# A causal convolution of four taps as one chain of three DVE instructions, on one Trainium2 core

## The chip, the core and the metric

One core of a Trainium2 chip runs the whole program. PE (TensorE) multiplies matrices into PSUM, DVE (VectorE), ACT (ScalarE) and POOL (GpSimd) work elementwise beside it, and SP (SyncE) issues most of the DMAs. Each engine takes its own instructions strictly in the order in which they were written, and semaphores hold an instruction until what it reads is there. The metric is the device time of one execution in microseconds (us).

## The reference

A trunk of two layers over 1024 frames of 1024 channels in float32. Layer 0 is chunked attention, layer 1 a gated DeltaNet, and a squared-ReLU MLP follows each. The part that matters here is the input of the DeltaNet layer: q, k and v (8 heads of 128 channels each) pass a depthwise causal convolution of four taps and a SiLU.

```python
CONV_K = 4
def causal_conv(x, w):
    """Depthwise causal conv. x: (B,S,Ch), w: (K,Ch); last tap hits the current frame."""
    S = x.shape[1]
    xp = jnp.pad(x, ((0, 0), (CONV_K - 1, 0), (0, 0)))
    y = xp[:, 0:S] * w[0]
    for j in range(1, CONV_K):
        y = y + xp[:, j:j + S] * w[j]
    return y
...
def gated_deltanet(h, w_in, conv_w, a_log, dt_bias, head_norm, w_o):
    proj = h @ w_in
    ...
    qkv = jax.nn.silu(causal_conv(qkv, conv_w))
    q, k, v = jnp.split(qkv, 3, axis=-1)
    ...
    o = chunk_gated_delta_rule(q, k, v, g, beta)
```

`chunk_gated_delta_rule` solves a unit lower triangular system in each chunk of 64 frames and then carries a 128x128 state through 16 chunks per head, one after the other.

## The kernel before

Activations lie transposed, channels on the 128 partitions and frames along the free dimension, in two halves of 512 frames (`HB`). A float32 product is made of three fp32r matmuls with operands split into a high and a low part (`whi`, `wlo`, `xs`), so a dense output tile of 128 channels and 512 frames takes 24 matmuls into a PSUM bank `acc`.

The DeltaNet stage (`deltanet`, `dn_run`) goes through a list of dense jobs: k of heads 0 to 7, then q and v of heads 0 to 2, then z, q and v by turns, the last z, and two panels of the output projection (`o`). Each of the 32 jobs ahead of the output projection has 48 matmuls. After every dense matmul `dn_run` calls `turn`, which steps other tasks where their inputs are ready: `dn_evac` (this change), `dn_blocks` (the k by k products `U` of a head), `dn_solves` (the triangular solves, four heads at a time, 31 steps of a product `ft` and a reduction `fz` on DVE), `dn_inverses`, `dn_prep_keys`, `dn_prep_values`, `dn_prep_queries`, `dn_scans` (16 dependent steps per head: PE makes `s`, DVE makes `vn`, PE, DVE makes the next state `st`), `dn_outs` and `dn_reload`.

Which task steps when is decided while the program is built, by a planned clock (`Clock`): each instruction is charged a planned cost (on DVE, 0.08 + 512/850 us for one scalar_tensor_tensor of 512 columns), a task becomes ready at the planned end of its last step, and tasks whose priority is 1 or more wait while DVE or ACT is planned more than 2 us ahead of PE. So a change of one task's instructions moves the others' places in all queues. Ring buffers (`xp`, `cy`, `cz`, two of each) are taken and given back on the same clock.

`dn_evac` handles one half head. For q, k and v it scales the bank into `xp` (with three columns carried over from the first half), multiplies tap 3 into `y` (a `cy` tile) and tap 1 into `z` (a `cz` tile) on ACT, adds tap 2 to `y` and tap 0 to `z` on DVE, sums `y` and `z` on POOL, and applies SiLU on ACT into `k`, `qT` or `vT`. For k of heads 4 to 7 (`POOLED`) the division of work is another: POOL sums taps 3 and 1, ACT makes a third product (tap 0), DVE adds tap 2 alone, and POOL sums again. There are 48 half heads, 8 of them pooled.

All instructions of this stage are recorded through one wrapper at line 163, so the profile shows L163 for them, and they are told apart by the names of their tiles (`cy<-xp,convw` is an ACT product, `cy<-xp,convw,cy` a DVE tap, `cy<-cy,cz` the POOL sum). After the change that wrapper stands at line 162.

Of the kernel before, what the change touches and what calls it, by code (L numbers as in the profile page):

```python
# [10 lines left out]
AF = mybir.ActivationFunctionType  # L11
ALU = mybir.AluOpType
# [8 lines left out]
HB = 512  # L21
# [13 lines left out]
ATT = (3, 2, 0.5, 1, 1, 0.7, 0.6)  # L35
RINGS = {"pt": 2, "po": 2, "sp": 1, "pr": 6, "bias": 3, "thi": 4, "tlo": 3, "oh": 1, "ot": 2}
ENGINES = {"dn_solves": ("vector",), "dn_decays": ("scalar",)}
POOLED = (4, 5, 6, 7)


def wide(col, p, n):
# [166 lines left out]
class Trunk:  # L208
# [1862 lines left out]
    def dn_evac(self, c, h, half, ps):  # L2071

        nc = self.nc
        s = slice(half * HB, (half + 1) * HB)
        if c == "z":
            if half == 0:
                if h == 1:
                    yield from self.until("solve", 1)
                if h >= 2:
                    yield from self.until("out", h - 2)  # L2080
                self.heads[c, h] = self.dn_out_of(c, h)
            while (c, h) not in self.heads:
                yield
            t = self.heads[c, h][:, s]
            nc.vector.tensor_tensor(t, ps, self.R[:, s], ALU.mult)
            self.give("acc", ps)
            yield
            nc.scalar.activation(t, t, AF.Silu)
        else:
            w = self.convw[:, 8 * "qkv".index(c) + h]  # L2090
            xp = yield from self.take("xp")
            if half == 0:
                nc.vector.memset(xp[:, 0:3], 0.0)
            else:
                nc.vector.tensor_copy(xp[:, 0:3], self.edge[:, HB : HB + 3])
            self.edge = xp
            nc.vector.tensor_tensor(xp[:, 3 : 3 + HB], ps, self.R[:, s], ALU.mult)
            self.give("acc", ps)
            yield
            yt = yield from self.take("cy")  # L2100
            zt = yield from self.take("cz")
            y, z = yt[:, :HB], zt[:, :HB]
            nc.scalar.activation(y, xp[:, 3 : 3 + HB], AF.Copy, scale=w[:, 3:4])
            nc.scalar.activation(z, xp[:, 1 : 1 + HB], AF.Copy, scale=w[:, 1:2])
            yield
            if c == "k" and h in POOLED:
                nc.gpsimd.tensor_tensor(z, y, z, ALU.add)
                yield
                nc.scalar.activation(y, xp[:, 0:HB], AF.Copy, scale=w[:, 0:1])
                nc.vector.scalar_tensor_tensor(z, xp[:, 2 : 2 + HB], w[:, 2:3], z, ALU.mult, ALU.add)  # L2110
            else:
                nc.vector.scalar_tensor_tensor(y, xp[:, 2 : 2 + HB], w[:, 2:3], y, ALU.mult, ALU.add)
                nc.vector.scalar_tensor_tensor(z, xp[:, 0:HB], w[:, 0:1], z, ALU.mult, ALU.add)
            self.give("xp", xp)
            yield
            nc.gpsimd.tensor_tensor(y, y, z, ALU.add)
            self.give("cz", zt)
            yield
            if half == 0:
                for need in self.dn_room(c, h):  # L2120
                    yield from self.until(*need)
                self.heads[c, h] = self.dn_out_of(c, h)
            while (c, h) not in self.heads:
                yield
            nc.scalar.activation(self.heads[c, h][:, s], y, AF.Silu)
            self.give("cy", yt)
            self.silu_at = self.clock.at["scalar"]
        if half == 1:
            self.mark(c, h)
# [532 lines left out]
```

## Time and profile before

| what | value |
|---|---|
| three runs | 2573.45, 2576.89, 2579.90 us; median 2576.89 us |
| the profiled execution | 2579.18 us, of which the span from the first to the last instruction is 2577.4 us |
| PE | busy 2472.7 us, 96% |
| DVE | busy 1914.8 us, 74% |
| POOL | busy 1298.2 us, 50% |
| ACT | busy 1210.1 us, 47% |
| DeltaNet stage | about 1206 to 1860 us of the span |

Busy times are shares of the span over all stages, whose limits differ. PE's ends are modelled, so a busy PE isn't PE at its peak. A row of an engine's timeline has its start, its duration, the operation, the tiles (`out<-in`), the shape and a count; what stands in brackets is the idle time just ahead of it and what ended that. The chain of waits goes back from the last instruction, at each step to what released it.

### The profile page before, as it was taken

What the parts mean: (1) busy time and instruction counts of PE and PEld (TensorE: products, weight loads), DVE (VectorE), ACT (ScalarE), POOL (GpSimd) and SP (SyncE); (2) the same over time, 40 slices, a digit from 0 to 9 for tenths busy, and PEclk for the clock granted to TensorE, in tenths of its full rate; (3) what the DMA queues carried; (4) which work ended last, traced back from release to release, by engine and by line L of the source; (5) the groups of instructions that cost most, each with busy time, mean ns of one, the idle gap of its engine ahead of it and who ended that gap; (6) DMA issues with size and microseconds to landing.
All of it is one profiled execution on the core that took longest, in us unless ns stands there. A gap on an engine that the chain in (4) does not pass through costs nothing.

```text
span 2577.4 us, 36731 instructions
## 1 busy us (share of the span) xinstructions
PE 2472.7 (96%) x12638; PEld 2063.6 (80%) x12638; DVE 1914.8 (74%) x3297; ACT 1210.1 (47%) x2269; POOL 1298.2 (50%) x1090
## 2 busy tenths in 40 slices
PE   8999999999999999998888999999899999999997
PEld 6888888787888788886677788888787888787885
DVE  6665556677878788877578976666678787778877
ACT  6666567535555433334673333333335555433333
POOL 2444355515677476556464333332314766466656
PEclk9999999999999999999998999999999999999998
DMA  4222224424555976743343121122323555967742
GB/s 160 68 65 73 71 84 129 140 82 167 210 203 215 358 233 227 249 147 111 116 142 106 55 82 60 59 85 94 119 98 143 208 209 200 345 235 253 249 160 82
DMA packets 193082, 392.43 MB, mean 152 GB/s; under 512 B 54960, under 2 KB 61552, under 8 KB 192896
## 3 DMA queue, kind: packets, MB, share of 16 engines
q1 hardware_dynamic: 176048, 355.46, 41.0%
q10 hardware_dynamic: 16848, 34.63, 3.4%
q8 instruction: 100, 1.64, 0.3%
q14 instruction: 86, 0.70, 0.1%
HBM read 254.06 MB, written 127.57 MB: 148 GB/s over the span
## 4 chain that ended last, share of the span: by engine, by line
PE 61%; DVE 11%; DMA 3%; issue 3%; ACT 1%; POOL 1%; SPq 0%; ACTq 0%; DVEq 0%; POOLq 0%
PE y L1008 24%; PE z L1008 11%; PE acc L163 9%; PE acc L1008 6%; PE tp L163 4%; PE s L163 3%; DVE ft L163 2%; PE acc L279 1%; PE acc L277 1%; PE acc L278 1%; DVE x L1512 1%; DMA wraw<-in_w_up_dram 1%; DVE wlo L1014 1%; DVE fz L163 1%; DVE xs L393 1%
## 5 line engine op out<-in xcount | busy, mean ns | idle before, releaser
L163 PE MATMUL acc<-xs,whi 128*128 128x512 f32 x1808 | 633.9, 414 | 10.4 <-DVE xp L163 9.8
L163 PEld LDWEIGHTS acc<-xs,whi 128*128 128x128 f32 x1808 | 334.8, 192 | 60.0 <-DVE xp L163 6.1
L163 PE MATMUL acc<-xs,wlo 128*128 128x512 f32 x896 | 369.6, 413 | 2.1 <-POOL wlo L163 2.1
L1008 PE MATMUL y<-xs,whi 128*128 128x512 f32 x1008 | 312.0, 390 | 5.2 <-DVE x L1512 1.8
L163 POOL TENSOR_TENSOR wlo<-wraw,whi 128x512 fp32r<-128x512 f32 x126 | 167.7, 1331 | 246.3 <-ACT whi L163 197.3
L1023 POOL TENSOR_TENSOR s<-wraw 128x256 f32<-128x256 f32 (+1 forms) x93 | 89.4, 962 | 352.9 <-DVE a L1014 171.9
L1014 DVE TENSOR_TENSOR wlo<-wraw,whi 128x512 fp32r<-128x512 f32 (+1 forms) x182 | 209.4, 1151 | 27.3 <-ACT whi L1017 27.3
L1008 PEld LDWEIGHTS y<-xs,whi 128*128 128x128 f32 x1008 | 189.2, 188 | 47.1 <-DVE x L1512 2.6
L1017 ACT ACTIVATE whi<-wraw 128x512 fp32r<-128x512 f32 (+2 forms) x191 | 146.5, 767 | 123.8 <-PE y L1008 86.6
L1008 PE MATMUL y<-xs,wlo 128*128 128x512 f32 x504 | 197.0, 391 | 6.2 <-DVE wlo L1014 6.2
L1008 PE MATMUL y<-xs,a 128*128 128x512 f32 x732 | 189.0, 394 | 10.0 <-DVE x L1512 9.8
L1017 ACT ACTIVATE a<-s 128x256 fp32r<-128x256 f32 x122 | 63.8, 524 | 281.5 <-PE y L1008 141.7
L163 PEld LDWEIGHTS acc<-xs,wlo 128*128 128x128 f32 x896 | 172.6, 193 | 27.0 <-POOL wlo L163 2.5
L1512 DVE TENSOR_TENSOR x<-y,x 128x512 f32<-128x512 f32 x240 | 165.0, 688 | 36.8 <-PE y L1008 28.6
L1008 PEld LDWEIGHTS y<-xs,a 128*128 128x128 f32 x732 | 136.6, 189 | 44.5 <-DVE x L1512 14.2
L1008 PE MATMUL acc<-xs,whi 128*128 128x512 f32 x528 | 162.9, 390 | 0.0
L1008 PE MATMUL y<-xs,ahi 128*128 128x512 f32 x512 | 159.2, 392 | 0.7 <-ACT nt L1201 0.4
L1090 DVE TENSOR_TENSOR c<-c 128x512 fp32r<-128x512 f32 x112 | 132.8, 1203 | 28.5 <-POOL c L1020 28.5
L163 POOL TENSOR_SCALAR pr<-pr,rs 128x640 f32<-128x640 f32 (+4 forms) x128 | 88.1, 692 | 129.4 <-DVE rs L163 96.7
L1008 PE MATMUL z<-xs,whi 128*128 128x512 f32 x480 | 148.8, 391 | 0.0
L163 POOL TENSOR_TENSOR cy<-cy,cz 128x512 f32<-128x512 f32 x48 | 68.9, 1435 | 146.7 <-DVE cz L163 124.3
L163 DVE CUSTOM_DVE_ANT_0 pr<-sp,bias 128x640 f32<-128x640 f32 (+4 forms) x128 | 83.8, 655 | 63.8 <-PE sp L163 62.8
(340 smaller groups left out, 6295.2 us busy)
## 6 DMA issues: line engine op xcount, KB each, us to landing
xs<-gt SPq DMA_DIRECT2D x256, 256.0 KB, 4.9
gt<-c SPq DMA_DIRECT2D x112, 512.0 KB, 3.0
wraw<-in_w_up_dram SPq DMA_DIRECT2D x64, 512.0 KB, 3.5
wraw<-in_w_down_dram SPq DMA_DIRECT2D x64, 512.0 KB, 4.4
r<-gr SPq DMA_DIRECT2D x88, 256.0 KB, 3.4
wraw<-in_w_in_dram SPq DMA_DIRECT2D x32, 512.0 KB, 3.4
gr<-ssum ACTq DMA_DIRECT2D x62, 256.0 KB, 3.2
wraw<-in_w_qkv_dram SPq DMA_DIRECT2D x30, 512.0 KB, 3.4
```

The costliest lines, as they stand in the source:

```text
L163: return call(*args, **more)
L277: nc.tensor.matmul(ps, hi[:, k], xh, start=(k == 0), stop=False)
L278: nc.tensor.matmul(ps, hi[:, k], xl, start=False, stop=False)
L279: nc.tensor.matmul(ps, lo[:, k], xh, start=False, stop=(k == KT - 1))
L393: self.nc.vector.scalar_tensor_tensor(lo, x, w, hi.bitcast(F32), ALU.mult, ALU.subtract)
L1008: nc.tensor.matmul(ps, w[:, k], x, start=bool(first and f), stop=bool(last and e), skip_group_check=True)
L1014: self.nc.vector.tensor_tensor(lo, src, hi.bitcast(F32), ALU.subtract)
L1017: self.nc.scalar.activation(hi, src, AF.Copy)
L1023: self.nc.gpsimd.tensor_tensor(out, x, y, ALU.add)
L1090: nc.vector.tensor_tensor(t[z][:, HB:].bitcast(F32R), t[z][:, HB:], t[z][:, :HB], ALU.subtract)
L1512: nc.vector.tensor_tensor(x, ps, x, ALU.add)
```

## The change

A half head's convolution becomes one product on ACT (tap 3, into `cy`) and three scalar_tensor_tensor instructions on DVE that add taps 2, 1 and 0 to the same tile, each reading what the one ahead of it wrote. The second ACT product, the two sums on POOL and the special way of k's heads 4 to 7 go. `cz` isn't taken by the convolution any more (`dn_reload` still uses it).

```diff
-POOLED = (4, 5, 6, 7)
...
             yt = yield from self.take("cy")
-            zt = yield from self.take("cz")
-            y, z = yt[:, :HB], zt[:, :HB]
+            y = yt[:, :HB]
             nc.scalar.activation(y, xp[:, 3 : 3 + HB], AF.Copy, scale=w[:, 3:4])
-            nc.scalar.activation(z, xp[:, 1 : 1 + HB], AF.Copy, scale=w[:, 1:2])
-            yield
-            if c == "k" and h in POOLED:
-                nc.gpsimd.tensor_tensor(z, y, z, ALU.add)
-                yield
-                nc.scalar.activation(y, xp[:, 0:HB], AF.Copy, scale=w[:, 0:1])
-                nc.vector.scalar_tensor_tensor(z, xp[:, 2 : 2 + HB], w[:, 2:3], z, ALU.mult, ALU.add)
-            else:
-                nc.vector.scalar_tensor_tensor(y, xp[:, 2 : 2 + HB], w[:, 2:3], y, ALU.mult, ALU.add)
-                nc.vector.scalar_tensor_tensor(z, xp[:, 0:HB], w[:, 0:1], z, ALU.mult, ALU.add)
+            yield
+            for n in (2, 1, 0):
+                nc.vector.scalar_tensor_tensor(y, xp[:, n : n + HB], w[:, n : n + 1], y, ALU.mult, ALU.add)
             self.give("xp", xp)
-            yield
-            nc.gpsimd.tensor_tensor(y, y, z, ALU.add)
-            self.give("cz", zt)
             yield
```

Counted over the program, ACT loses 56 products (104 become 48) and 2 table loads (20 become 18), POOL loses 56 sums, and DVE gains 56 scalar_tensor_tensor (88 become 144).

Three places show how the order moves. The first is DVE at the start of the first solve, where the convolutions of k's last heads stand among the solve's steps (`ft`, `fz`) and the `U` products. Before:

```order
L163 TENSOR_TENSOR U_13195<-tp_13196,vT_12994 128x512
L163 TENSOR_TENSOR ft_13174<-fz_12321,fu_12320 128x9
L163 TENSOR_REDUCE fz_12321<-ft_13174 128x3
L163 TENSOR_TENSOR ft_13174<-fz_12321,fu_12320 128x16
L163 TENSOR_REDUCE fz_12321<-ft_13174 128x4
L163 TENSOR_TENSOR U_13195<-tp_13225,vT_12994 128x512
L163 SCALAR_TENSOR_TENSOR cz_13183<-xp_13160,convw,cz_13183 128x512
L163 TENSOR_TENSOR ft_13174<-fz_12321,fu_12320 128x25
```

And of the change:

```order
L162 TENSOR_TENSOR fu_12320<-fu_12320,ry_13096 128x1024
L162 SCALAR_TENSOR_TENSOR cy_13174<-xp_13156,convw,cy_13174 128x512 x3
L162 TENSOR_TENSOR ft_13210<-fz_12321,fu_12320 128x1
L162 TENSOR_REDUCE fz_12321<-ft_13210 128x1
L162 TENSOR_TENSOR U_13140<-tp_13217,vT_12997 128x512
L162 TENSOR_TENSOR ft_13210<-fz_12321,fu_12320 128x4
L162 TENSOR_REDUCE fz_12321<-ft_13210 128x2
```

Where one tap stood ahead of a solve step, three stand in a row. Counting the dense matmuls ahead of it in PE's order, the first solve's first step moves from 342 to 367 and its last from 541 to 594; the second solve's first step moves from 599 to 682, and the first head's first scan step from 613 to 691.

The second place is POOL over the same stretch (`wlo` is a weight's low part, `row` and `vT` hold decays to be masked). Before:

```order
L163 TENSOR_TENSOR wlo_12824<-wraw_12673,whi_12823 128x512
L163 TENSOR_TENSOR cz_12887<-cy_12886,cz_12887 128x512
L163 TENSOR_TENSOR wlo_12925<-wraw_12761,whi_12924 128x512
L163 TENSOR_TENSOR cz_12929<-cy_12928,cz_12929 128x512
L163 TENSOR_TENSOR row_12915<-row_12915,mask 128x512
L163 TENSOR_TENSOR cy_12886<-cy_12886,cz_12887 128x512
```

And of the change:

```order
L162 TENSOR_TENSOR wlo_12893<-wraw_12779,whi_12892 128x512 x2
L162 TENSOR_TENSOR row_12927<-row_12927,mask 128x512 x2
L162 TENSOR_TENSOR vT_12997<-vT_12997,mask 128x512 x2
L162 TENSOR_TENSOR wlo_13035<-wraw_12844,whi_13034 128x512 x2
```

Only weights and masks are left on POOL there.

The third place is PE at the end of the stage, where head 7 is scanned (`s`, with `vn`, `st`, `kd`, `WQ` and `qk`) beside the last dense matmuls (`acc`). Before:

```order
L163 MATMUL s_3767_17862<-st_17846,WQ_17613 128x128
L163 MATMUL acc_17844<-xs_11813,whi_17570 128x512 x2
L163 MATMUL acc_17844<-xs_11813,wlo_17571 128x512
L163 MATMUL acc_17844<-xs_11815,whi_17570 128x512 x2
L163 MATMUL acc_17844<-xs_11815,wlo_17571 128x512
L163 MATMUL s_3779_17887<-vn_12245,kd_17498 128x128
L163 MATMUL s_3767_17862<-vn_12245,qk_12251 128x128
L163 MATMUL acc_17844<-xs_11817,whi_17570 128x512 x2
L163 MATMUL acc_17844<-xs_11817,wlo_17571 128x512
```

And of the change:

```order
L162 MATMUL s_3736_17832<-st_17826,WQ_17582 128x128
L162 MATMUL s_3740_17840<-vn_12244,kd_17465 128x128
L162 MATMUL s_3736_17832<-vn_12244,qk_12251 128x128
L162 MATMUL s_3742_17852<-st_17846,WQ_17582 128x128
L162 MATMUL s_3743_17857<-vn_12245,kd_17465 128x128
L162 MATMUL s_3742_17852<-vn_12245,qk_12251 128x128
L162 MATMUL s_3745_17864<-st_17861,WQ_17582 128x128
```

Several scan steps now follow each other with no dense matmul between them. Head 7's scan begins behind 1530 dense matmuls instead of 1476, and 20 scan steps instead of 9 stand behind the 1536th.

## The prediction

> **What bounds the kernel now.** The chain of waits comes first, since it tells which engine's work ended last. Over the whole program:
>
> ```profile
> PE 61%; DVE 11%; DMA 3%; issue 3%; ACT 1%; POOL 1%; SPq 0%; ACTq 0%; DVEq 0%; POOLq 0%
> ```
>
> PE carries the program and DVE is second, with shares of 61% and 11%; ACT and POOL, which lose work here, have 1% each. Such shares are averages, so the next view is the busy time by stretches of the DeltaNet stage, to which the change is confined (columns: the stretch, its length, PE, PEld, DVE, ACT and POOL busy with their counts, PE's granted clock, the DMA share, GB/s):
>
> ```profile
> 1220.00:1420.00 200.00, 172.81 (x848) 143.13 (x847) 147.52 (x268) 114.29 (x201) 107.11 (x80) 0.91 0.41 121
> 1420.00:1540.00 120.00, 113.97 (x815) 96.13 (x814) 103.96 (x221) 45.03 (x91) 44.14 (x33) 1.00 0.22 66
> 1540.00:1820.00 280.00, 273.11 (x1883) 239.74 (x1882) 183.00 (x474) 105.18 (x233) 88.10 (x65) 0.99 0.23 75
> 1820.00:1860.00 40.00, 32.66 (x154) 25.36 (x153) 25.06 (x62) 15.20 (x31) 10.46 (x10) 0.96 0.45 151
> ```
>
> The reader is to see four limits. From 1220 to 1420 (k's jobs, the first solve) PE is idle for 27 of 200 us and runs at a clock of 0.91, which costs 9% of its 173 busy us, another 16: some 43 us are lost there, with no engine full. From 1420 to 1540 (the second solve) DVE is busy 87%. From 1540 to 1820 PE is the bound, 98% busy, and DVE has a third free. In the last 40 us PE waits again, for head 7's scan.
>
> What PE waits for in the first stretch is read from the waits of the stage (us in total, times, longest) and from single rows of PE:
>
> ```profile
> PE acc L163 <- DVE xp L163: 9.8, 2, 5.9
> 1363.52 0.63 ACT L163 ACTIVATE qT<-cy 128x512 f32<-128x512 f32 x1 [4.83 <-POOL cy L163]
> 1364.72 3.57 PE L163 MATMUL tp<-ones,nt 128*128 128x1 f32 x16 [3.43 <-ACT nt L163]
> 1368.73 0.63 PE L163 MATMUL acc<-xs,wlo 128*128 128x512 f32 x1
> 1369.15 1.05 PE L163 MATMUL acc<-xs,whi 128*128 128x512 f32 x2
> 1385.87 0.39 PE L163 MATMUL acc<-xs,wlo 128*128 128x512 f32 x1
> 1386.10 0.62 PE L163 MATMUL acc<-xs,whi 128*128 128x512 f32 x2
> 1395.13 2.07 PE L163 MATMUL tp<-qT,kn 128*128 128x128 f32 x8 [6.12 <-DVE vb L163]
> ```
>
> Four gaps hold 9.8 + 3.43 + 6.12 = 19.4 us of the 27. Two wait for a bank that DVE has still to empty into `xp`, one for q's squares (`nt`), which ACT makes behind q's SiLU, which waited for the sum on POOL, one for DVE's `vb`. Behind the 3.43 us gap the clock is low: a matmul starts 0.42 us after the one ahead (1368.73 to 1369.15), against 0.23 later (1385.87 to 1386.10).
>
> **The change, part by part.** The rows of what is removed and added (count: shortest/median/longest ns):
>
> ```profile
> L163 DVE SCALAR_TENSOR_TENSOR cz<-xp,convw,cz x48: 737/745/1766, 1222.0 to 1761.6; 128x512 f32<-128x512 f32 x48
> L163 DVE SCALAR_TENSOR_TENSOR cy<-xp,convw,cy x40: 734/748/1710, 1221.3 to 1761.0; 128x512 f32<-128x512 f32 x40
> L163 ACT ACTIVATE cz<-xp,convw x48: 705/708/712, 1221.2 to 1759.2; 128x512 f32<-128x512 f32 x48
> L163 POOL TENSOR_TENSOR cy<-cy,cz x48: 1258/1287/2792, 1222.8 to 1763.5; 128x512 f32<-128x512 f32 x48
> L163 POOL TENSOR_TENSOR cz<-cy,cz x8: 1256/1297/1740, 1289.0 to 1344.9; 128x512 f32<-128x512 f32 x8
> ```
>
> POOL loses 56 x 1.29 = 72 us, ACT 56 x 0.71 = 40 us. Neither is a bound, so by themselves they give nothing; they count where something waits behind them. DVE gains 56 instructions, and the price of one depends on whether it waits for the one ahead:
>
> ```profile
> 1358.61 1.41 DVE L163 TENSOR_TENSOR ft<-fz,fu 128x529 f32<-128x529 f32 x1
> 1360.05 0.71 DVE L163 TENSOR_REDUCE fz<-ft 128x23 f32<-128x529 f32 x1
> 1360.67 0.74 DVE L163 SCALAR_TENSOR_TENSOR cy<-xp,convw,cy 128x512 f32<-128x512 f32 x1
> 1361.33 0.75 DVE L163 SCALAR_TENSOR_TENSOR cz<-xp,convw,cz 128x512 f32<-128x512 f32 x1
> 1362.00 0.68 DVE L163 TENSOR_TENSOR U<-tp,vT 128x512 f32<-128x512 f32 x1
> ```
>
> The two taps of before are independent and start 0.66 us apart, less than they last. `fz` reads what `ft` wrote and starts 1.44 us behind it, 0.03 after its end. A chain of three taps so holds DVE for 0.78 + 0.78 + 0.66 = 2.22 us, against 1.32 before: 0.9 more in each of 40 half heads, and 2.22 - 0.66 = 1.56 more in the 8 pooled ones, 48.5 us in all. Queued behind the second and third tap are solve steps at the first place shown, and whatever waits for those waits 0.9 to 1.56 us longer. The planner charges 3 x 0.682 = 2.05 us, so it is only 0.17 short.
>
> The Trainium skill (VectorE: DVE Perf Modes, section "The DRAIN you can't avoid") states that a chain costs the same as free instructions, since the pipe empties after each anyway. By that rule the added cost would be 56 x 0.745 = 42 us instead of 48.5; the rows above show free ones overlapping by 0.08 us, and the sum goes by them.
>
> Where does it fall? DVE's taps by stretch, for `cz`, of which there is one in each half head (second column group: DVE busy and count):
>
> ```profile
> 1220.00:1420.00 200.00, 21.77 (x24) 17.00 (x24) 46.26 (x32) 0.91 0.41 121
> 1420.00:1540.00 120.00, 5.95 (x8) 5.67 (x8) 13.02 (x9) 1.00 0.22 66
> 1540.00:1820.00 280.00, 13.29 (x16) 11.69 (x17) 20.50 (x16) 0.99 0.23 75
> ```
>
> Step 1, **the first stretch**: 16 x 0.9 + 8 x 1.56 = 27 us more on DVE, which is busy 147.5 of 200 there, so it fits; and 32 POOL sums go. What a sum does to DVE is seen here:
>
> ```profile
> 1336.56 1.53 POOL L163 TENSOR_TENSOR cz<-cy,cz 128x512 f32<-128x512 f32 x1
> 1337.38 1.11 DVE L163 TENSOR_TENSOR ft<-fz,fu 128x225 f32<-128x225 f32 x1
> 1340.11 0.57 DVE L163 TENSOR_TENSOR ft<-fz,fu 128x256 f32<-128x256 f32 x1
> ```
>
> The product over 225 columns took 1.11 us, and ended 0.4 us after the POOL sum beside it; the larger one over 256 columns took 0.57. So a sum can hold up a solve step by 0.6 us or more, and a half head now crosses between engines three times instead of four. Of the lost 43 us I take back the gap behind the POOL sum with half of its slow clock (3.4 + 2), half of the two `xp` gaps (5), and something under half of the `vb` gap (2.6), 13 us. The bounds are 0 (the late transfers and long ACT queues stay) and 27 (all idle time).
>
> Step 2, **the second solve**: 8 x 0.9 = 7 us on a DVE that is 87% busy. It is hidden only if it lands in the 16 us that DVE has free there; I take 7. The bounds are 0 and 20, the latter if the 8 pooled half heads' 12.5 us also stand in a solve's way. The order bears this out in kind: the second solve starts behind 682 dense matmuls, not 599.
>
> Step 3, **from 1540 on**: 16 x 0.9 = 14 us lie beside PE, since DVE has 97 of 280 us free. No cost; should that cover go, 14 us.
>
> Step 4, **the end**:
>
> ```profile
> 1797.38 0.21 DVE L163 COPY vn<-vb 64x128 f32<-64x128 f32 x1
> 1815.65 0.40 PE L163 MATMUL acc<-xs,whi 128*128 128x512 f32 x1
> 1823.44 0.29 DVE L163 TENSOR_TENSOR vn<-vb,s 64x128 f32<-64x128 f32 x1
> 1825.31 0.28 DVE L163 TENSOR_TENSOR vn<-vb,s 64x128 f32<-64x128 f32 x1
> 1825.81 0.38 PE L163 MATMUL s<-vn,kd 128*128 128x128 f32 x2
> 1826.03 0.39 PE L163 MATMUL s<-vn,qk 128*128 128x128 f32 x2
> 1840.04 0.29 DVE L163 TENSOR_TENSOR vn<-vb,s 64x128 f32<-64x128 f32 x1 [1.25 <-PE s L163]
> ```
>
> Head 7's scan starts with the copy at 1797.38 and makes its last `vn` at 1840.04: 15 steps of 2.84 us among dense matmuls. A step with none between took 1.87 (1823.44 to 1825.31). In the new order it starts behind 1530 dense matmuls, which before was 1815.65, from where the last `vn` was 24.4 us away. At 2.2 us a step it will be 33 away: 8.6 us more. Against that, 11 scan steps now stand behind the 1536th dense matmul that stood ahead of it; each has three matmuls, 0.21 us apart, so 11 x 0.63 = 6.9 us of PE work leave the stretch where PE is the bound. Net 2 us; with steps of 1.87 and 2.84 us, -3 and +11.
>
> The sum: -13 + 7 + 0 + 2 = -4 us. The profiled execution took 2579.2 us, so 2575; it lies 2.3 us above the median of 2576.9, so the forecast is **2573 us**.
>
> **The rivals.**
>
> *Faster, by more than 0.3%.* The waits of the first stretch go almost wholly and the pooled order was the hindrance: -23 there, +3 at the second solve, +1 at the end, -19 in all, 2558 us. For it: no engine is full in that stretch, so it is waits that cost, and the change makes the chain shorter on two engines. Against it: of the gaps, only the one behind q's SiLU names the sum on POOL, and DVE gets 27 us more to do in the same stretch. A rule of the Trainium skill works this way (SBUF — State Buffer, section "Who interferes with whom"): a DVE instruction with two SBUF inputs and a POOL instruction that reads SBUF block each other for the whole instruction. The 1.11 us row agrees; the same rule also makes the new taps, with two SBUF inputs, collide with POOL's remaining weights.
>
> *Slower, by more than 0.3%: DVE becomes the bound.* Place: the two solves, whose steps stand in DVE's queue between the taps. It decides once DVE's work per dense matmul exceeds PE's; at 1420 to 1540 the 104 us rise to 111, against PE's 114, so the margin is 3 us. If it tips, step 2 costs 20; heads fall further behind the dense work, so the end costs 11 to 13, and step 1 yields 10: about +22, 2599 us. For it: every head's scan starts later in the new order. Against it: the planner has already spread the solves, and POOL holds DVE up less.
>
> *The change doesn't reach the path.* Conv work is beside PE everywhere and the new order is as good as the old: 2577 us. It has the forecast's sign and is counted with it.
>
> **How the numbers follow.** About 0.3%, 8 us, is what a measurement of this kernel can tell from no change. Within it, with the forecast and the last rival: 0.37, its own range 2569 to 2584. Faster: 0.33. Slower: 0.30. The steps' bounds add to -30 and +31, but are hardly met together. The range for 8 in 10 takes in both rivals' times but for their outer parts: 2555 to 2598.
>
> **What would show it.** Step 1: between 1220 and 1420 PE's idle time falls from 27 to about 15 us and its clock rises above 0.91; wrong if a bank waits for `xp` more than twice. Steps 2 and 3: taps start 0.78 us apart inside a chain, and DVE in the second solve is above 90%; wrong if PE is idle there for more than 15 us. Step 4: head 7's `vn` stand about 2.2 us apart and the stage's last 40 us have more idle time on PE. The forecast fails if the solve's steps, taken one by one, still last 1.1 us with the sums gone, or if PE's stretch after the second solve isn't 98% busy any more.

## The result, and the profile after

| | before | with the chain |
|---|---|---|
| median of the timed runs | 2577.1 us (4 runs) | 2599.61 us (2598.75 to 2599.8, 4 runs) |
| ratio to before | 1 | 1.0085, 95% interval 1.0073 to 1.0097 |
| span of the profiled execution | 2577.4 us | 2597.0 us |

The change is slower by 22 us. That is 1.6 us above the range given, and not the small gain that was forecast.

The busy time by stretches of the stage, for the change (columns as in the prediction):

```profile
1220.00:1420.00 200.00, 172.53 (x801) 142.27 (x799) 156.28 (x276) 91.28 (x165) 63.59 (x46) 0.93 0.40 117
1420.00:1540.00 120.00, 110.60 (x791) 91.60 (x791) 104.53 (x216) 33.37 (x69) 31.50 (x23) 0.93 0.20 59
1540.00:1820.00 280.00, 271.71 (x1884) 237.13 (x1883) 195.41 (x493) 97.48 (x217) 69.45 (x50) 0.99 0.21 68
1820.00:1860.00 40.00, 33.90 (x159) 26.50 (x158) 24.29 (x78) 13.16 (x34) 8.22 (x6) 0.79 0.46 160
```

POOL and ACT have much less to do in the first stretch (POOL 63.6 us instead of 107.1), and PE gained nothing from it: 172.5 us busy, as before. From 1540 to 1820 PE is as full as it was. The last 40 us look alike here only because the stage now ends some 20 us later; they are opened up below.

Where the time is lost is read from single events. The first two rows are the solves' reductions, the other two the scans' `vn`, of before and of the change (count: shortest/median/longest ns, start of the first and of the last):

```profile
L163 DVE TENSOR_REDUCE fz<-ft x62: 154/422/1156, 1320.6 to 1499.1; 128x1 f32<-128x1 f32 x2, 128x2 f32<-128x4 f32 x2, 128x3 f32<-128x9 f32 x2, 128x4 f32<-128x16 f32 x2
L163 DVE TENSOR_TENSOR vn<-vb,s x120: 265/291/293, 1432.1 to 1840.0; 64x128 f32<-64x128 f32 x120
```

```profile
L162 DVE TENSOR_REDUCE fz<-ft x62: 154/422/1156, 1330.4 to 1519.4; 128x1 f32<-128x1 f32 x2, 128x2 f32<-128x4 f32 x2, 128x3 f32<-128x9 f32 x2, 128x4 f32<-128x16 f32 x2
L162 DVE TENSOR_TENSOR vn<-vb,s x120: 268/291/294, 1453.9 to 1859.5; 64x128 f32<-64x128 f32 x120
```

The first solve starts 9.8 us later, the second ends 20.3 us later, and the last `vn` comes 19.5 us later; 2.3 us of each were there already when the stage began. From the last reduction to the last `vn` it took 340.9 us before and 340.1 now. Nothing was lost or won behind the second solve: it is a train that left some 18 us late.

The dense matmuls were hardly late when their jobs ended. The 1536th, the last ahead of the output projection, starts at 1817.5 before and at 1821.1 with the change, 1.3 us later counted from the stage's start (at the 1200th it was 9.7). The 1632nd, in the output projection, starts at 1858.9 and 1879.0, 17.8 us later. PE ran out of work that doesn't need the last heads, and waited for the train. One stretch near the end, before and then the change:

```profile
1829.00:1847.00 18.00, 16.94 (x78) 13.70 (x78) 11.70 (x33) 6.37 (x14) 3.85 (x3) 0.91 0.26 85
```

```profile
1829.00:1847.00 18.00, 13.64 (x57) 10.55 (x56) 9.55 (x34) 3.95 (x12) 1.89 (x1) 0.69 0.28 113
```

With the change only scan steps and a few transposes are on PE there, and the granted clock falls to 0.69 in the mean (0.50 from 1836 to 1850). The steps themselves become longer. Rows of DVE and then of PE in it:

```profile
1820.07 0.21 DVE L162 COPY vn<-vb 64x128 f32<-64x128 f32 x1
...
1830.98 0.28 DVE L162 TENSOR_TENSOR vn<-vb,s 64x128 f32<-64x128 f32 x1 [0.64 <-PE s L162]
1832.83 0.29 DVE L162 TENSOR_TENSOR vn<-vb,s 64x128 f32<-64x128 f32 x1 [0.64 <-PE s L162]
...
1837.24 0.29 DVE L162 TENSOR_TENSOR vn<-vb,s 64x128 f32<-64x128 f32 x1 [0.47 <-PE s L162]
1839.72 0.28 DVE L162 TENSOR_TENSOR vn<-vb,s 64x128 f32<-64x128 f32 x1 [0.95 <-PE s L162]
...
1859.47 0.29 DVE L162 TENSOR_TENSOR vn<-vb,s 64x128 f32<-64x128 f32 x1
```

```profile
1832.34 0.46 PE L162 MATMUL s<-st,WQ 128*128 128x128 f32 x2 [0.31 <-ACT o L162]
...
1838.91 0.77 PE L162 MATMUL s<-st,WQ 128*128 128x128 f32 x2
```

A scan step lasts 1.85 us at first, and 2.48 us after the clock has dropped; the same pair of matmuls takes 0.46 and then 0.77 us.

**Why the first solve starts later.** DVE's rows from the load of the solve's blocks to its first step, before:

```profile
1304.70 1.76 DVE L163 SCALAR_TENSOR_TENSOR cz<-xp,convw,cz 128x512 f32<-128x512 f32 x1 [1.74 <-POOL cz L163]
1306.38 0.18 DVE L163 TENSOR_SCALAR frt<-fu 128x32 f32<-128x32 f32 x1
...
1315.61 0.74 DVE L163 SCALAR_TENSOR_TENSOR cz<-xp,convw,cz 128x512 f32<-128x512 f32 x1
1316.27 1.22 DVE L163 TENSOR_TENSOR fu<-fu,ry 128x1024 f32<-128x1024 f32 x1
...
1320.42 0.14 DVE L163 TENSOR_TENSOR ft<-fz,fu 128x1 f32<-128x1 f32 x1
```

And with the change, with two rows of POOL below:

```profile
1310.45 4.22 DVE L162 SCALAR_TENSOR_TENSOR cy<-xp,convw,cy 128x512 f32<-128x512 f32 x3 [2.81 <-ACT cy L162]
1314.58 0.18 DVE L162 TENSOR_SCALAR frt<-fu 128x32 f32<-128x32 f32 x1
...
1319.13 2.33 DVE L162 SCALAR_TENSOR_TENSOR cy<-xp,convw,cy 128x512 f32<-128x512 f32 x3
...
1324.24 1.22 DVE L162 TENSOR_TENSOR fu<-fu,ry 128x1024 f32<-128x1024 f32 x1
1325.37 4.50 DVE L162 SCALAR_TENSOR_TENSOR cy<-xp,convw,cy 128x512 f32<-128x512 f32 x3
1329.80 0.57 DVE L162 TENSOR_TENSOR ft<-fz,fu 128x1 f32<-128x1 f32 x1
```

```profile
1309.10 2.53 POOL L162 TENSOR_TENSOR vT<-vT,mask 128x512 f32<-128x512 f32 x2 [3.08 <-DMA vT<-grows]
1324.60 3.70 POOL L162 TENSOR_TENSOR row<-row,mask 128x512 f32<-128x512 f32 x2 [8.54 <-DMA row<-grows]
```

Where two single taps stood (these are pooled half heads), there are now three blocks of three, 11.1 us together, and each stands directly in the way of the solve. The undisturbed block lasts 2.33 us; the two that run beside work on POOL (the masks shown, then a weight's low part behind the first pair and two small products behind the second) last 4.22 and 4.50.

**Why it lasts longer.** From its first `ft` to the end of its 31st `fz` the first solve took 73.1 us before and 81.6 with the change. Counted from the start of each tap to the start of DVE's next instruction, taps hold 11.6 us of that before and 19.6 now. Against it, the 31 products `ft` became shorter, from 32.5 to 28.6 us in all.

### The profile page after: what moved, and what is told of

Read it like the earlier page. It is cut to its first block, busy times and chain, and to the rows that moved or that the text cites. A ratio compares the mean times of both kernels' runs of the same rounds, so it can differ in the third digit from the quotient of the medians.

```text
span 2597.0 us, 36618 instructions
## 1 busy us (share of the span) xinstructions
PE 2484.4 (96%) x12638; PEld 2068.1 (80%) x12638; DVE 1947.9 (75%) x3353; ACT 1173.6 (45%) x2211; POOL 1228.7 (47%) x1034
## 4 chain that ended last, share of the span: by engine, by line
PE 37%; DVE 8%; DMA 2%; issue 2%; ACT 1%; POOL 1%; SPq 0%; ACTq 0%; DVEq 0%; POOLq 0%
PE y L1007 12%; PE acc L162 8%; PE z L1007 6%; PE tp L162 3%; PE acc L1007 3%; PE s L162 3%; DVE cy L162 2%; DVE ft L162 1%; DVE fz L162 1%; PE acc L278 1%; PE acc L276 1%; PE acc L277 1%; DMA xs<-gt 1%; DMA wraw<-in_w_down_dram 0%; DMA wraw<-in_w_up_dram 0%
## 5 line engine op out<-in xcount | busy, mean ns | idle before, releaser
L1013 DVE TENSOR_TENSOR wlo<-wraw,whi 128x512 fp32r<-128x512 f32 (+1 forms) x182 | 208.0, 1143 | 27.5 <-ACT whi L1016 27.5
L162 PEld LDWEIGHTS acc<-xs,wlo 128*128 128x128 f32 x896 | 172.0, 192 | 26.5 <-POOL wlo L162 1.3
L162 DVE SCALAR_TENSOR_TENSOR cy<-xp,convw,cy 128x512 f32<-128x512 f32 x144 | 126.0, 876 | 25.7 <-ACT cy L162 22.1
```

What stands on the lines that cost most here:

```text
L162: return call(*args, **more)
L1013: self.nc.vector.tensor_tensor(lo, src, hi.bitcast(F32), ALU.subtract)
```

## The experiments

"Plan" means the order that the kernel's own planner writes; `charge` adds an instruction's cost to the planner's clock without issuing one. Times in the table come from each kernel's trace; each run is shifted so that the first matmul of the stage, one of the gates', lies at before's 1200.0. The trace is that of one execution, and not always of a middling one: it took 2575.4 us for m3 (median 2584.4), 2575.1 for m6 (2567.5) and 2587.7 for h_before (2594.5). The median of before lay between 2574.9 and 2577.5 us beside the different kernels, and each ratio is to the runs beside it. "Lasts" is from the first `ft` to the end of the 31st `fz`.

| kernel | median us | ratio to before, 95% interval | first solve starts | lasts | second solve ends | last `vn` |
|---|---|---|---|---|---|---|
| before | 2577.1 | 1 | 1320.4 | 73.1 | 1500.2 | 1840.0 |
| the change | 2599.6 | 1.0085 (1.0073 to 1.0097) | 1327.5 | 81.6 | 1518.3 | 1857.2 |
| e1 old order, chain | 2591.0 | 1.0059 (1.0044 to 1.0074) | 1318.6 | 78.3 | 1504.4 | 1847.8 |
| e2 new order, old work | 2598.5 | 1.0086 (1.0070 to 1.0102) | 1334.2 | 77.7 | 1520.4 | 1858.9 |
| e3 late second solve | 2598.5 | 1.0088 (1.0070 to 1.0106) | 1320.4 | 73.6 | 1523.0 | 1857.1 |
| e6 chain in three steps | 2590.9 | 1.0058 (1.0042 to 1.0074) | 1329.0 | 81.2 | 1515.9 | 1852.9 |
| e4 chain for q, v | 2594.2 | 1.0071 (1.0050 to 1.0092) | 1318.9 | 74.2 | 1507.0 | 1856.2 |
| e5 chain for k | 2594.8 | 1.0065 (1.0049 to 1.0082) | 1326.5 | 80.4 | 1513.7 | 1852.2 |
| h_before | 2594.5 | 1.0061 (1.0039 to 1.0082) | 1319.1 | 71.8 | 1483.9 | 1846.2 |
| h_after | 2607.2 | 1.0115 (1.0096 to 1.0134) | 1326.6 | 82.2 | 1490.0 | 1854.8 |
| n1 control | 2587.7 | 1.0045 (1.0030 to 1.0060) | 1321.0 | 74.9 | 1505.7 | 1845.0 |
| m1 chain, edit of n1 | 2604.2 | 1.0113 (1.0093 to 1.0133) | 1326.3 | 82.0 | 1517.5 | 1861.4 |
| n2 control | 2589.3 | 1.0044 (1.0027 to 1.0061) | 1318.9 | 73.7 | 1502.5 | 1848.0 |
| m2 chain, edit of n2 | 2605.1 | 1.0120 (1.0096 to 1.0144) | 1327.7 | 82.0 | 1513.9 | 1854.5 |
| m3 before, pause 0.11 | 2584.4 | 1.0025 (1.0012 to 1.0037) | 1317.7 | 67.5 | 1485.9 | 1834.4 |
| a1 chain, pause 0.11 | 2597.2 | 1.0076 (1.0061 to 1.0091) | 1323.2 | 84.6 | 1510.3 | 1853.8 |
| a2 three steps, re-planned | 2585.5 | 1.0032 (1.0020 to 1.0043) | 1328.7 | 79.1 | 1514.7 | 1845.6 |
| m6 before, re-planned | 2567.5 | 0.9965 (0.9952 to 0.9977) | 1319.0 | 76.2 | 1498.5 | 1822.7 |
| m7 chain, edit of m6 | 2593.1 | 1.0067 (1.0052 to 1.0082) | 1322.0 | 80.9 | 1511.4 | 1853.2 |
| m8 chain for q, v, edit of m6 | 2599.5 | 1.0094 (1.0077 to 1.0111) | 1318.7 | 83.2 | 1512.7 | 1857.3 |

### Work and order taken apart (e1, e2)

The change does two things at once: it puts 56 more taps on DVE, and it makes the planner write another order. e1 has before's order with the chain in it:

```diff
-            nc.scalar.activation(z, xp[:, 1 : 1 + HB], AF.Copy, scale=w[:, 1:2])
+            charge("scalar", "activation", (z, xp, AF.Copy), {"scale": w[:, 1:2]})
...
-                nc.vector.scalar_tensor_tensor(y, xp[:, 2 : 2 + HB], w[:, 2:3], y, ALU.mult, ALU.add)
-                nc.vector.scalar_tensor_tensor(z, xp[:, 0:HB], w[:, 0:1], z, ALU.mult, ALU.add)
+                charge("vector", "scalar_tensor_tensor", (y, xp), {})
+                charge("vector", "scalar_tensor_tensor", (z, xp), {})
+            for n in (2, 1, 0):
+                nc.vector.real.scalar_tensor_tensor(
+                    y, xp[:, n : n + HB], w[:, n : n + 1], y, ALU.mult, ALU.add)
...
-            nc.gpsimd.tensor_tensor(y, y, z, ALU.add)
+            charge("gpsimd", "tensor_tensor", (y, y, z, ALU.add), {})
```

> The order of before on every engine, word for word, with the chain's work in it: the planner is charged as before, the second product and the POOL sums are not issued, and three dependent taps stand where two stood. Theory 'order': the loss comes from where the new plan puts the solve's steps, so here it is gone: within 6 us of before, 2571 to 2583, with the second solve ending within 5 us of before's 1499. Theory 'work': three taps hold DVE 0.9 to 1.56 us longer ahead of solve steps wherever they stand, so most of the 22 us are here: 2592 or more, second solve ending at 1513 or later.

e2 is the reverse: three taps are charged, and before's instructions are issued in their place.

```diff
+            for n in (2, 1, 0):
+                charge("vector", "scalar_tensor_tensor", (y, xp), {})
...
+                dve.scalar_tensor_tensor(y, xp[:, 2 : 2 + HB], w[:, 2:3], y, ALU.mult, ALU.add)
+                dve.scalar_tensor_tensor(z, xp[:, 0:HB], w[:, 0:1], z, ALU.mult, ALU.add)
+            pool.tensor_tensor(y, y, z, ALU.add)
```

> The counterpart: the order of the change for all other instructions, with before's work (two or three ACT products, two or one taps, POOL sums) where the chain stood. Theory 'order': slower than before by most of the 22 us, 2592 to 2602, since the scans still stand where the new plan put them. Theory 'work': near before, 2583 or less, since DVE's 48 us are gone again. If both this and the counterpart are slower by 8 to 14 us, each has a half.

Measured: 2591.0 and 2598.5. By their ratios the chain's work in the old order costs 15 us, and the old work in the new order the whole 22. They don't add up: 15 and 22 against 22 for both. The same views as above, of e1 and of e2:

```profile
L163 DVE TENSOR_REDUCE fz<-ft x62: 154/422/1156, 1319.1 to 1503.5; 128x1 f32<-128x1 f32 x2, 128x2 f32<-128x4 f32 x2, 128x3 f32<-128x9 f32 x2, 128x4 f32<-128x16 f32 x2
L163 DVE TENSOR_TENSOR vn<-vb,s x120: 265/291/293, 1433.0 to 1848.1; 64x128 f32<-64x128 f32 x120
```

```profile
L163 DVE TENSOR_REDUCE fz<-ft x62: 153/422/1155, 1334.0 to 1518.9; 128x1 f32<-128x1 f32 x2, 128x2 f32<-128x4 f32 x2, 128x3 f32<-128x9 f32 x2, 128x4 f32<-128x16 f32 x2
L163 DVE TENSOR_TENSOR vn<-vb,s x120: 267/291/294, 1454.7 to 1858.5; 64x128 f32<-64x128 f32 x120
```

What follows from e1: without room planned for them, the taps stand in DVE's queue in front of steps that are ready, and the loss grows bit by bit: 4 us at the end of the second solve, 8 at the last `vn`. The time is 1 us short of what the theory 'work' asked for, while the solve's end fits the theory 'order'; neither holds whole.

e2 shows less than it seems to. It gave the time of the theory 'order', but it has a wait of its own: in its eight pooled half heads the tap stands at the place of the chain, where POOL's sum isn't ready. DVE waits 38.9 us for those sums, 6.2 in before. Three of these waits, 13.6 us, lie just ahead of the first solve:

```profile
1314.42 0.75 DVE L2113 SCALAR_TENSOR_TENSOR cz<-xp,convw,cz 128x512 f32<-128x512 f32 x1 [5.57 <-POOL cz L2111]
1324.06 0.75 DVE L2113 SCALAR_TENSOR_TENSOR cz<-xp,convw,cz 128x512 f32<-128x512 f32 x1 [4.36 <-POOL cz L2111]
1333.17 0.75 DVE L2113 SCALAR_TENSOR_TENSOR cz<-xp,convw,cz 128x512 f32<-128x512 f32 x1 [3.67 <-POOL cz L2111]
```

So its late first solve (1334.2, later than the change's 1327.5) need not come from the order, and what the new order costs alone is not shown.

### Is it one chain to the end (e3)?

```diff
-            yield from self.sleep(G["sl_solve"])
+            yield from self.sleep(G["sl_solve"] + 20.0 * g)
```

> Before, with one number changed: the second solve sleeps 20 us longer on the planner's clock ahead of its first step (its end is planned 17 us later). No instruction is added. Theory 'one chain from the second solve to the end': from the end of that solve to the last vn it took 341 us before and 340 after the change, so it takes 336 to 346 here too, and the time rises by what the solve is late: 2590 to 2600. Theory 'PE is the bound there' (as the prediction had it): the scans have slack beside the dense matmuls, and the time stays within 5 us of before.

```profile
L163 DVE TENSOR_REDUCE fz<-ft x62: 153/422/1156, 1322.3 to 1523.6; 128x1 f32<-128x1 f32 x2, 128x2 f32<-128x4 f32 x2, 128x3 f32<-128x9 f32 x2, 128x4 f32<-128x16 f32 x2
L163 DVE TENSOR_TENSOR vn<-vb,s x120: 266/291/294, 1430.3 to 1858.8; 64x128 f32<-64x128 f32 x120
```

Measured: 2598.5, 22 us slower with not one instruction more. The last `vn` starts 335.2 us behind the last reduction (341 before). The edit draws a new plan too, but the dense matmuls keep their places within some 5 us: counted from the stage's start, the 1200th starts 5.1 us later than in before and the 1536th 3.9 us earlier, and the first solve is as before. A late second solve, with the work of before, gives the time of the change. The reading that PE alone is the bound from 1540 on falls.

### The chain in three steps (e6)

```diff
             for n in (2, 1, 0):
                 nc.vector.scalar_tensor_tensor(y, xp[:, n : n + HB], w[:, n : n + 1], y, ALU.mult, ALU.add)
-            self.give("xp", xp)
-            yield
+                if n == 0:
+                    self.give("xp", xp)
+                yield
```

> The change, with each of the three taps a step of its own of the task, so that the planner may put a solve or scan step between two taps. The work is that of the change. If the loss is that a chain is queued as one block ahead of the dependent steps, the first solve's 80.5 us fall back towards 72 and the time comes within 6 us of before (2571 to 2583). If it is the added 48 us of DVE work as such, it stays at 2592 or more.

Measured: 2590.9, between the two forecasts. The first solve starts as late as in the change and lasts as long (81.2 us); only the second is shorter. Other instructions do stand between the taps there, so it is not the block as such that delays the first solve.

### k alone, q and v alone (e5, e4)

```diff
+            if c == "k":
+                yt = yield from self.take("cy")
+                y = yt[:, :HB]
...
+                for n in (2, 1, 0):
...
+            else:
+                yt = yield from self.take("cy")
+                zt = yield from self.take("cz")
...
```

> The chain for k alone, q and v as before. Theory 'the first solve is planned too late': its order up to the first solve is that of the change, so the first solve starts at 1328 or later and the second ends at 1510 or later: 2590 to 2600. Theory 'taps among the dependent steps': 24 us of the 48 on DVE are left, and all of them ahead of or inside the first solve, so 2577 to 2587. Both parts slower by 15 or more would mean that the parts don't add, and that the later of two chains decides.

> The chain for q and v alone; k's 16 half heads as before (POOL sums, heads 4 to 7 pooled). Theory 'the first solve is planned too late': the first solve's place depends on k alone, so it starts within 4 us of before's 1320 and at least half of the loss is gone: 2577 to 2587. Theory 'taps among the dependent steps': 32 half heads with a longer block of taps still stand among the solves' and scans' steps, so most of the loss is here: 2590 to 2605.

Measured: 2594.8 (k) and 2594.2 (q, v; the condition reversed). Both lose 17 us. With k's chain the first solve is 6.1 us late (8 or more were expected) and lasts 7.3 us longer, and the second ends behind 1510, as expected. With q's and v's chain the first solve is as before, but the second takes 83.5 instead of 76.4 us and the scans behind it 349 instead of 340. Taken by themselves, neither part is free, and the parts don't add. This is where a third theory came up: that any new plan loses some 15 us, because before's places happen to fit the chip.

### The second solve's front moved ahead (h_before, h_after)

In before, 30 us lie between the end of the first solve and the first step of the second. The edit makes the front of each solve (loads, reciprocal roots, scalings) a task of its own:

```diff
+            self.add(G["dn_front%d" % odd], self.dn_solve_front(odd))
...
+    def dn_solve_front(self, g):
+
+        nc, db = self.nc, self.db
...
+            self.front[g] = fu, Z
+            self.mark("front", g)
...
+            yield from self.until("front", g)
+            fu, Z = self.front.pop(g)
```

> Before, with the front of each solve (the loads of its blocks, the reciprocal roots and the two scalings) as a task of its own, so that the second solve's front runs beside the first solve instead of behind it; no instruction is added. In before 31 us lie between the two solves. Theory 'one chain from the second solve to the end': the second solve ends some 13 us earlier, the last vn 336 to 346 us behind it, and the time falls by up to 13, to 2563 to 2572. Theory 'PE is the bound behind the solves': the time stays within 5 us of before, or rises since DVE has more to do in the first solve.

> The same edit on the change. Theory 'one chain from the second solve to the end': the 34 us between the solves shrink by 15 or more, and so does the loss: 2578 to 2588. Theory 'PE is the bound behind the solves' or a loss from DVE work as such: 2595 to 2605.

Measured: 2594.5 and 2607.2, both slower than their partners. A miss for the theory of one chain: the second solve ended 16 us earlier in `h_before`, but the last `vn` followed 362 us behind its end, not 340. The dense matmuls fell behind meanwhile: counted from the stage's start, the 1200th started 30.1 us later than in before. With the dense work late, the heads' q and v are late, and the scans that need them can't start; that this is what held them is likely, and not shown. `h_after` lies above both of its forecasts. Its second solve ends 28 us earlier than in the change and the last `vn` only 2.4, though its 1200th dense matmul is just 0.9 us later. What holds the scans there stays open. So the chain from the second solve to the end has a length of 340 us only in plans where nothing else is late: delaying it costs (e3), and ending its solve earlier gained nothing.

### Controls: another plan, the same work (n1, n2)

```diff
-'dkeys': 4
+'dkeys': 2.97
```

> A control: before, with one planner priority changed (the tasks that load and scale the keys, 4 to 2.97, so that they go ahead of other tasks of equal readiness). No instruction is added or taken away, only places change from the first solve on. Theory 'what stands in the queue is what costs' (taps in front of dependent steps, or a first solve placed late): nothing of that is changed, so 2572 to 2584. Rival 'the places of before happen to fit the chip, and any new plan loses some 15 us': 2587 to 2600, as in the four re-planned kernels so far.

n2 changes `'dn_inverses': 2` to `3.34`.

> A second control of the same kind: before, with the priority of the inverses changed from 2 to 3.34, so that they yield to other tasks. No instruction is added or taken away. The same two forecasts: 2572 to 2584 if only late solves and blocks of taps cost; 2587 to 2600 if any new plan does.

Measured: 2587.7 and 2589.3. No instruction was added, and 11 to 12 us are lost. So a good part of any single comparison is the luck of the plan, and a difference of 15 us between two kernels with different orders doesn't by itself tell what their instructions cost. e1 has before's order, and e3's trace shows which step moved; e4, e5, e6 and the two kernels with the front ahead can't be read more finely than that.

### Pairs: the same planner edit with and without the chain

> The change with the first control's edit (the keys' priority 4 to 2.97). That control took 2587.6 with before's work. If the chain has a cost of its own beside the loss that any new plan brings, this is slower than its partner by 8 or more: 2596 to 2612. If all of the 22 us are the luck of the plan, the two differ by chance alone: 2580 to 2595.

> The change with the second control's edit (the inverses' priority 2 to 3.34). That control took 2589.2 with before's work. A cost of the chain's own: 2597 to 2612. Luck of the plan alone: 2582 to 2597.

> The change, with the planner's pause between engines 0.11 instead of 0.15 us, which gives another plan in which the second solve stands earlier. The work is that of the change. Theory 'the place of the second solve sets the end': the second solve ends earlier than 1519 by 4 us or more and the time falls by as much below 2599, the last vn still 336 to 346 us behind it. Rival 'the added DVE work sets it': 2595 to 2603 wherever the solve stands.

> Before, with the planner's pause between engines 0.11 instead of 0.15 us, the partner of the change planned with that pause, which took 2597.2. A cost of the chain's own: this one is faster by 8 or more, 2575 to 2589. Luck of the plan alone: 2588 to 2602, as likely above as below its partner.

> Before, planned with a pause between engines of 0.08 us and a DVE lead of 2.22 instead of 2.0 us, the plan with the shortest end on the planner's own clock that I found for before's work. If that clock tells a good plan from a bad one, at or below before: 2565 to 2577. If it can't, as with the two controls: 2582 to 2595.

> The change with the planner edit that made before's work faster than before (2567.5). Four pairs so far, the same planner edit with before's work and with the chain, differ by 12.7 to 22.5 us, the chain slower in each. A cost of the chain's own holds under this plan too: 2578 to 2590. If a plan that fits hides it: 2562 to 2573.

m1, m2 and m3 came out as a cost of the chain's own asked. In a1 the second solve ended 8 us earlier than in the change, but the time fell by 2.4 us only: the rival's forecast, and against 'the place of the second solve sets the end'. m6 was faster than before, as the planner's clock had it. m7 lies above both of its forecasts, so a plan that fits doesn't hide the cost.

The edits are m1: that of n1; m2: that of n2; a1 and m3: `'c_other': 0.15` to `0.11`; m6 and m7: `'c_other'` to `0.08` and `'dload0': 2.0` to `2.22`.

| plan | before's work | chain | difference | end of first solve later by | last `vn` later by |
|---|---|---|---|---|---|
| as it is | 2577.1 | 2599.6 | 22.5 | 15.6 | 17.1 |
| keys first | 2587.7 | 2604.2 | 16.6 | 12.4 | 16.4 |
| inverses later | 2589.3 | 2605.1 | 15.9 | 17.1 | 6.5 |
| pause 0.11 | 2584.4 | 2597.2 | 12.8 | 22.6 | 19.5 |
| pause 0.08, lead 2.22 | 2567.5 | 2593.1 | 25.6 | 7.7 | 30.5 |
| front ahead | 2594.5 | 2607.2 | 12.7 | 17.9 | 8.6 |
| mean | 2583.4 | 2601.1 | 17.7 | 15.6 | 16.4 |

All six differences have one sign, 12.7 to 25.6 us, mean 17.7. The plans with before's work spread over 27 us, those with the chain over 14. So the chain has a cost of its own, about 18 us, and the measured 22 is that and, as it seems, some of before's luck (its plan is 6 us better than the mean of its six). The traces say the same more sharply: from the stage's start to the program's end, the execution with the chain is longer by 17.2, 16.1, 16.6, 16.9, 26.5 and 17.0 us in the order of the table. Only a1 and a2 (below) use plans chosen for the chain; what a longer search for such plans would give is not shown.

In every pair the first solve starts later, by 3.0 to 8.8 us, and lasts longer, by 4.7 to 17.1 us. In all six, taps hold DVE longer inside it (by 7.3 to 15.0 us), and its products `ft` take 3.9 to 6.9 us less. By its end the mean loss is 15.6 us, and at the last `vn` 16.4. But pair by pair the one doesn't give the other: where the first solve ends 22.6 us later, the last `vn` is 19.5 later, and where it ends 7.7 later, 30.5. In two pairs ("inverses later", "front ahead") 10.1 and 8.4 us of the loss arise behind the last `vn`; the granted clock from 1860 to 1880 is 0.79 and 0.82 there, against 1.00 and 0.91 in the partners. So the cost is shown, and that the taps delay the first solve is shown; how the delay travels to the end is not the same in every plan.

m6 also shows that a better plan than before's exists for before's work: 2567.5 us, ratio 0.9965 (0.9952 to 0.9977), the fastest kernel of this study. With the same edit the chain takes 2593.1. Their two rows each, m6 and then m7:

```profile
L163 DVE TENSOR_REDUCE fz<-ft x62: 154/421/1156, 1326.1 to 1504.1; 128x1 f32<-128x1 f32 x2, 128x2 f32<-128x4 f32 x2, 128x3 f32<-128x9 f32 x2, 128x4 f32<-128x16 f32 x2
L163 DVE TENSOR_TENSOR vn<-vb,s x120: 266/291/294, 1443.9 to 1829.5; 64x128 f32<-64x128 f32 x120
```

```profile
L162 DVE TENSOR_REDUCE fz<-ft x62: 154/422/1155, 1321.6 to 1509.2; 128x1 f32<-128x1 f32 x2, 128x2 f32<-128x4 f32 x2, 128x3 f32<-128x9 f32 x2, 128x4 f32<-128x16 f32 x2
L162 DVE TENSOR_TENSOR vn<-vb,s x120: 266/291/294, 1441.2 to 1852.2; 64x128 f32<-64x128 f32 x120
```

In m6 the scans take 325 us from the last reduction to the last `vn`, instead of 341: most of its gain lies there, not in the solves. (These rows are not shifted; 6.8 us in this execution of m6 lie ahead of the stage.)

### Two last attempts

a2 is the chain in three steps, planned with `'c_small': 0.08` and `'dn_prep_queries': 3.07`:

> The change with its taps as three steps of the task (2591 as it stood), planned with a pause of 0.08 instead of 0.12 us between DVE steps and the queries ahead of the values. The work is that of the change. If a plan made for this work is all that is missing, the second solve ends by 1505 and the time is at or below before's, 2565 to 2580; if the added DVE work costs wherever it stands, 2588 or more.

Measured: 2585.5, neither of the two: the best with the chain, still slower than before (1.0020 to 1.0043), and 18 us slower than m6. The second solve ends at 1514.7, late as ever; the scans behind it are quicker, 331 us from its end to the last `vn` instead of 340.

m8 is e4 with m6's edit:

> As the last, with the chain for q and v alone and k as before. In all kernels with the chain in k the first solve started at 1323 to 1330 and lasted 79 to 85 us, in those without it 1316 to 1321 and 67 to 78 (but for the one in the change's order). If k's taps ahead of the first solve are the own cost, this kernel starts that solve before 1322 and is within 6 us of its partner without any chain: 2562 to 2574. If q's and v's taps cost as much: 2576 or more.

Measured: 2599.5, which is slower than with the chain everywhere. The first solve started early, as expected, but lasted 83.2 us. That k's taps alone are the own cost falls with it. How the 18 us divide between k, q and v stays open: every division comes with a plan of its own, whose luck is as large as what is to be divided.

## Why the prediction was wrong

**The price of a chain was right.** Forecast were starts 0.78 us apart, so 2.31 us from the first start to the last end; the undisturbed block lasted 2.33, and so did the median of the 48. Not in the price was what POOL does to it: the mean tap grew from 858 ns (34.5 and 41.0 us for the 40 and 48 taps) to 876, the mean block lasted 2.70 us, and the first 16, of k, 3.00. The time in which a tap runs on DVE grew from 72.3 to 126.0 us, 53.7 more against 48.5 forecast.

```profile
L162 DVE SCALAR_TENSOR_TENSOR cy<-xp,convw,cy 128x512 f32<-128x512 f32 x144 | 126.0, 876 | 25.7 <-ACT cy L162 22.1
```

The rule of the Trainium skill that was weighed against this change (SBUF — State Buffer, section "Who interferes with whom") agrees with the rows: a tap has two SBUF inputs, and beside POOL's masks and what followed them three took 4.22 and 4.50 us. That POOL lost 56 sums didn't make DVE's taps shorter.

**Step 1 failed: "it fits".** The 27 us on DVE in the first stretch were counted as hidden, since DVE was busy 147.5 of 200 us. DVE is one queue in a fixed order, and the solve in that queue is the start of a chain that ends late. Free time on DVE elsewhere in the stretch is of no use to a step that stands behind a block of taps. Instead of -13, the first solve's end came 15.6 us later (15.6 in the mean of six pairs too). One gain did come: without the sums on POOL the solve's products are shorter. The one over 225 columns, shown with 1.11 us, now is this row:

```profile
1351.61 0.56 DVE L162 TENSOR_TENSOR ft<-fz,fu 128x225 f32<-128x225 f32 x1
```

But it is 3.9 us in the whole solve, less than the 8.0 more that the taps take in it. PE got none of its gains: its idle time in the stretch is 27.5 us, as before (15 was forecast), the clock rose by 0.02 only, and it waits for `xp` as long as it did, three times instead of twice, which the prediction had named as a sign of being wrong:

```profile
PE acc L162 <- DVE xp L162: 9.5, 3, 5.3
```

**Step 2 named the right mechanism at the wrong place.** The second solve was to cost 7 us; from its first `ft` to its end it took 76.4 us before and 76.3 with the change, and DVE is at 87% as it was, not above 90%. What was lost, was lost ahead of it: 15.6 us by the end of the first solve, and 2.6 between the two.

**Step 3 held as a statement on PE** (271.7 of 280 us, 97%), and misled. A full PE in that stretch was read as the bound, so that nothing beside it would cost. e3 shows that the scans have little slack: a second solve 23 us late moved the last `vn` by 17 and the time by 22. The stage has two chains of nearly the same length, the dense matmuls and the solves with the scans behind them, and in the change the second sets the end. The busy share shows only the first.

**Step 4 saw the sign and missed the size.** Forecast were +2 us, as 8.6 for later scans less 6.9 for PE work taken out of the full stretch. The head's scan took 39.4 us (1820.07 to 1859.47), not 33, with 2.6 us a step instead of 2.2; and the credit was none, since PE, done with its dense jobs, only waited longer. The whole loss comes due here: at the 1536th dense matmul the change is 1.3 us behind before, at the 1632nd 17.8.

**The rivals.** The slower one had the time, 2599, and its rule that the heads fall behind the dense work and the end pays. Its place was wrong: it needed the second solve to tip, DVE above PE, and DVE didn't tip (104.5 us of work, 110.6 on PE). A late first solve was not among them. It stood in the order that was shown: first step behind 367 dense matmuls instead of 342, last behind 594 instead of 541. That was read as harmless, "the planner has already spread the solves". The range was cut too narrow as well: the steps' bounds add to +31, and leave out the 14 us of step 3, while the range ends 21 us above before.

## What to carry to other kernels

When a dependent chain shares an in-order engine with other work, find out first whether that chain or the busiest engine sets the end: delay the chain alone by a known amount and see whether the time follows. Moving work onto that engine then costs where it stands in the queue, even when the engine has a quarter of its time free.

Where a planner writes the order, any change of one task's instructions draws a new plan. Re-plan both kernels in the same few ways and compare in pairs: here single plans of the same work differed by up to 27 us, and only the pairs showed that the chain costs about 18.

## What the runs showed of the hardware

- PE's granted clock fell to 0.69 (0.50 from 1836 to 1850) where only scan steps and transposes were left on it, and the steps, which wait for each other, went from 1.85 to 2.48 us. In before the same 18 us had dense matmuls among them, and 0.91. Running out of work is so paid twice.
- Three dependent taps took 2.33 us alone and up to 4.50 beside masks and small products on POOL, though POOL had 56 instructions less in the stage. A solve's product over 225 columns took 1.11 us beside a sum on POOL, and 0.56 with the sum gone.
